# Where the low parts of the local q's weights are made: VectorE's subtraction, or a negation on ScalarE and an accumulating DMA

## The chip, the cores and the metric

The kernel runs on one core of one Trainium2 chip. The metric is the device time of one execution in microseconds (us); the kernel before took 945.75 us (median of 3 runs, 945.48 to 945.87). The engines have short names in the rows: PE is TensorE, the matrix engine (PEld is its loading of weights), DVE is VectorE, ACT is ScalarE, POOL is GpSimd, and SP is SyncE, which here only issues DMAs.

## The reference, cut to what matters

Two encoder layers over 256 tokens of width 1024 in float32. Each layer is a half-step feed-forward block, a mixer with two groups of attention heads that share one input projection, and a second half-step feed-forward block. The change touches the mixer's `sq`, the queries of the local (windowed) heads.

```python
def hybrid_mixer(x, cos, sin, mask, w_in, w_out, lam_vec, subln_g, sink, lambda_init):
    h = x @ w_in                      # columns: dq 512, dk 512, dv 512, sq 512, sk 128, sv 128
    dq, dk, dv, sq, sk, sv = ...
    dq, dk = apply_rope(dq), apply_rope(dk)
    y_diff = diff_attention(dq, dk, dv, lam, subln_g, lambda_init)
    sq, sk = apply_rope(sq), apply_rope(sk)
    y_swa = swa_sink_attention(sq, sk, sv, sink, mask)
    return concatenate([y_diff, y_swa]) @ w_out

for l in range(DEPTH):                # DEPTH = 2
    x = layer_norm(ALPHA * x + 0.5 * swiglu(x, ffn1_w_in[l], ffn1_w_out[l]), ...)
    x = layer_norm(ALPHA * x + hybrid_mixer(x, ..., w_in[l], w_out[l], ...), ...)
    x = layer_norm(ALPHA * x + 0.5 * swiglu(x, ffn2_w_in[l], ffn2_w_out[l]), ...)
```

## The kernel before

Every product is made from two parts of each operand: a high part, rounded to the matrix engine's format `float32r`, and a low part, the difference. A product is then three matmuls: high by high, high by low, low by high.

The weights come in pieces of 128 rows by 1024 columns (512 KB), 158 for each layer (index `i` in the list `srcs`, lines 134 to 149). The class `Weights` (line 58) makes piece `i`: SP issues the DMA into `raw` (line 80, 5 buffers), ACT copies `raw` into `wh` with rounding (line 82, 9 buffers), and DVE writes `wl = raw - wh` (line 83, 9 buffers). A piece is asked for 8 pieces before it is used (`LOOK`). So a new piece's `wh` and `wl` may be written only when PE has read the last of the piece that held the buffer before. The copy and the subtraction stand at a low priority for the scheduler that orders ACT and DVE; the order of PE is the order of the code.

In the mixer the order of PE's work is the table `ORDER` (line 48). `P sq 0 1` is one step of the projection of the local queries for the first half of the tokens: two k-tiles, that is one piece of weights, and six matmuls at lines 497 to 499 (`wh`, `wl`, `wh` again for each k-tile). In the list the pieces of `sq` are 80 to 83 in the first layer. Their first readers on PE stand far apart, with steps of `sk`, `dv` and the scores (`S d`, line 544) between them; the second half of the tokens reads the same pieces again later.

POOL has little to do: a power at line 297 in each layer norm and one at line 633 in each mixer's `diff_pv` (two a layer). No DMA is issued from POOL.

Of the kernel before, what the change touches and what calls it, by code (L numbers as in the profile page):

```python
# [9 lines left out]
F32 = mybir.dt.float32  # L10
# [4 lines left out]
ALU = mybir.AluOpType  # L15
# [36 lines left out]
P dv 0 1; T sk 1; G; A 0 0; T sq 0; P sq 1 1; V 0; S s 0; P sq 1 1; A 1 1; P sq 1 1; S s 0; A 1 0; Y 0; P sq 1  # L52
1; V 1; O 0 2; T sq 1; O 0 2; S s 1; B 0 0; B 0 1; Y 1; W 0 0; W 0 1; S s 1; O 1 1; O 0 4; B 1 0; B 1 1; O 1 2;
W 1 0; W 1 1; Z; O 1 5
"""


class Weights:


    def __init__(self, tc, pool, srcs):
        self.tc, self.nc, self.pool, self.srcs = tc, tc.nc, pool, srcs
        self.made = []

    def _make(self, i):
        nc = self.nc
        raw = self.pool.tile([P, 1024], F32, tag="raw", name=f"raw{i}", bufs=5)
        wh = self.pool.tile([P, 1024], F32R, tag="wh", name=f"wh{i}", bufs=9)
        wl = self.pool.tile([P, 1024], F32R, tag="wl", name=f"wl{i}", bufs=9)

        n = 512 if i < 3 else 1024
        src = self.srcs[i]

        rows = src if isinstance(src, tuple) else (src,)
        for c in range(0, 1024, n):
            s = slice(c, c + n)
            for q, r in enumerate(rows):
                h = P // len(rows)

                (nc.sync if i or c else nc.scalar).dma_start(raw[q * h : (q + 1) * h, s], r[:, s])  # L80
            with self.tc.high_priority(0 if i < 3 else -LATER):
                nc.scalar.copy(wh[:, s], raw[:, s])  # L82
                nc.vector.tensor_tensor(wl[:, s], raw[:, s], wh[:, s].bitcast(F32), ALU.subtract)  # L83
        self.made.append((wh, wl))

    def upto(self, n):
# [9 lines left out]
def encoder_kernel(  # L96
# [22 lines left out]
    nc = tc.nc  # L119
# [3 lines left out]
    wp = ctx.enter_context(tc.tile_pool(name="wp", bufs=1))  # L123
# [7 lines left out]
    dv = nc.vector  # L131


    srcs = []
    for l in range(DEPTH):
        srcs += [f1_b[l, k] for k in range(KT)]
        srcs += [f1_in[l, j, s] for j in range(JT - NB) for s in range(2)]
        srcs += [f1_out[l, k * P : (k + 1) * P, :] for k in range(JT)]
        for c in range(3):
            srcs += [m_in[l, c, q] for q in range(4)]  # L140
        srcs += [m_in2[l, q] for q in range(2)]
        srcs += [m_in[l, 3, q] for q in range(4)]
        srcs += [m_out[l, k * P : (k + 1) * P, :] for k in range(KT // 2)]

        srcs += [tuple(m_out[l, 512 + 256 * v + HD * n : 512 + 256 * v + HD * (n + 1), :] for v in range(2))
                 for n in range(KT // 2)]
        srcs += [f2_b[l, k] for k in range(KT)]
        srcs += [f2_in[l, j, s] for j in range(JT - NB) for s in range(2)]
        srcs += [f2_out[l, k * P : (k + 1) * P, :] for k in range(JT)]
    W = Weights(tc, wp, srcs)  # L150
    wi = 0


# [13 lines left out]
    def load_xt(k0, k1):  # L167
        k = slice(k0, k1)
        xr = tp.tile([P, 2, k1 - k0, P], F32, tag="tmp", name=f"xr{k0}")
        nc.sync.dma_start(xr, x_tr[:, :, k, :])  # L170
        xv = xr.rearrange("p t k c -> p k t c")
        dv.tensor_copy(xx[:, k, 0], xv)
        dv.tensor_tensor(xx[:, k, 1], xv, xx[:, k, 0].bitcast(F32), ALU.subtract)


    for k0, k1 in ((0, 1), (1, 2), (2, 4), (4, 6), (6, 8)):
        load_xt(k0, k1)
        W.upto(k1)
    x = []
# [129 lines left out]
    def ffn(l, n, last=False):  # L309
# [4 lines left out]
        def first(ts, mid=None):  # L314

            hp = [[ps.tile([P, 512], F32, tag="b", name=f"hb_{nm}_{t}{s}") for s in range(2)] for t in ts]
            for k in range(KT):
                wh, wl = W.get(wi + k)
                parts = ((0, wh, 0), (0, wl, 1), (1, wh, 2))
# [29 lines left out]
        def col(*js, flip=False):  # L349
# [3 lines left out]
            for j in js:  # L353

                hs = [ps.tile([P, 2, SEQ], F32, tag="b", name=f"h{'gu'[s]}_{nm}_{j}") for s in range(2)]
                tl = tp.tile([P, 2, SEQ], F32, tag="tl", name=f"tl_{nm}_{j}", bufs=2)
                ws = [W.get(wi), W.get(wi + 1)]
                wi += 2
# [67 lines left out]
        for k in range(JT - TAIL):  # L426
            w = W.get(wi)
            wi += 1
# [432 lines left out]
```

## Time and profile before

| | |
|---|---|
| median of 3 runs | 945.75 us (945.48 to 945.87) |
| the profiled execution | 946.11 us |
| its span, first to last instruction | 944.3 us |
| PE busy | 936.2 us (99%) |
| DVE busy | 657.2 us (70%) |
| ACT busy | 527.2 us (56%) |
| POOL busy | 18.8 us (2%) |
| DMA, mean over the span | 187 GB/s, 176.28 MB in all |

How to read it: the profiled execution's time is 1.8 us longer than its span, which is what lies ahead of the first and behind the last recorded instruction. Busy shares are averages over the whole span; what one stage waits for is read from rows of that stage. In the rows of a timeline the columns are start, duration, engine, line, operation, tiles (output, then inputs), shapes and count, and in brackets the idle time before it with the engine that ended it.

### The profile page before, as it was taken

What the parts mean: (1) busy time and instruction counts of PE and PEld (TensorE: products, weight loads), DVE (VectorE), ACT (ScalarE), POOL (GpSimd) and SP (SyncE); (2) the same over time, 40 slices, a digit from 0 to 9 for tenths busy, and PEclk for the clock granted to TensorE, in tenths of its full rate; (3) what the DMA queues carried; (4) which work ended last, traced back from release to release, by engine and by line L of the source; (5) the groups of instructions that cost most, each with busy time, mean ns of one, the idle gap of its engine ahead of it and who ended that gap; (6) DMA issues with size and microseconds to landing.
All of it is one profiled execution on the core that took longest, in us unless ns stands there. A gap on an engine that the chain in (4) does not pass through costs nothing.

```text
span 944.3 us, 13556 instructions
## 1 busy us (share of the span) xinstructions
PE 936.2 (99%) x5030; PEld 798.8 (85%) x5030; DVE 657.2 (70%) x1089; ACT 527.2 (56%) x906; POOL 18.8 (2%) x27
## 2 busy tenths in 40 slices
PE   9999999999999999999999999999999999999996
PEld 7888888888878888888889888888888889888885
DVE  6787664599887666664586666647998976666635
ACT  5768653346965666643346655543478656556520
POOL 0000000000100000000000000000001000000000
PEclk9999999999999999999999999999999999999999
DMA  8985676366526766676375666763763375666721
GB/s 311 317 274 179 185 227 193 119 235 171 145 73 200 238 179 183 196 223 200 115 247 197 196 184 198 222 189 112 240 175 112 108 238 182 191 193 193 214 66 44
DMA packets 51377, 176.28 MB, mean 187 GB/s; under 512 B 6512, under 2 KB 8304, under 8 KB 51312
## 3 DMA queue, kind: packets, MB, share of 16 engines
q1 hardware_dynamic: 51024, 175.03, 59.1%
q8 instruction: 39, 0.64, 0.3%
q10 hardware_dynamic: 288, 0.39, 0.1%
q14 instruction: 26, 0.21, 0.1%
HBM read 174.35 MB, written 1.05 MB: 186 GB/s over the span
## 4 chain that ended last, share of the span: by engine, by line
PE 99%; DVE 1%; issue 0%; DVEq 0%
PE acc L424 25%; PE hg L364 14%; PE hu L364 14%; PE hb L326 9%; PE hu L369 7%; PE hg L369 7%; PE ao L719 5%; PE pj_sq L497 1%; PE ss L544 1%; PE os L655 1%; PE pj_sq L499 1%; PE pj_sq L498 1%; PE pj_dq L497 1%; PE pj_dq L498 1%; PE tps L611 1%; PE pj_dv L499 1%
## 5 line engine op out<-in xcount | busy, mean ns | idle before, releaser
L83 DVE TENSOR_TENSOR wl<-raw,wh 128x1024 fp32r<-128x1024 f32 (+1 forms) x319 | 385.1, 1210 | 187.5 <-ACT wh L82 106.9
L82 ACT CAST wh<-raw 128x1024 fp32r<-128x1024 f32 (+1 forms) x319 | 332.9, 1047 | 211.2 <-PE acc L424 124.4
L424 PE MATMUL acc<-wh,g 128*128 128x512 f32 (+1 forms) x710 | 191.8, 388 | 0.0
L424 PEld LDWEIGHTS acc<-wh,g 128*128 128x128 f32 x710 | 132.9, 188 | 27.1
L364 PE MATMUL hg<-xx,wh 128*128 128x512 f32 x576 | 143.1, 390 | 0.0
L364 PE MATMUL hu<-xx,wh 128*128 128x512 f32 x576 | 142.3, 389 | 0.0
L364 PEld LDWEIGHTS hu<-xx,wh 128*128 128x128 f32 x576 | 108.1, 188 | 22.5
L364 PEld LDWEIGHTS hg<-xx,wh 128*128 128x128 f32 x576 | 106.6, 188 | 21.2
L424 PE MATMUL acc<-wl,g 128*128 128x512 f32 (+1 forms) x355 | 110.9, 387 | 0.0
L369 PE MATMUL hg<-xx,wl 128*128 128x256 f32 x576 | 81.0, 283 | 0.0
L369 PE MATMUL hu<-xx,wl 128*128 128x256 f32 x576 | 80.9, 283 | 0.0
L424 PEld LDWEIGHTS acc<-wl,g 128*128 128x128 f32 x355 | 66.7, 188 | 13.6
L369 PEld LDWEIGHTS hg<-xx,wl 128*128 128x128 f32 x576 | 75.4, 191 | 1.6
L369 PEld LDWEIGHTS hu<-xx,wl 128*128 128x128 f32 x576 | 74.3, 192 | 0.0
L326 PE MATMUL hb<-wh,xx 128*128 128x512 f32 x256 | 71.1, 396 | 0.0
L379 ACT COPY tl<-hg 128x256 f32<-128x256 f32 x72 | 26.8, 372 | 59.7 <-PE hg L364 57.9
L326 PEld LDWEIGHTS hb<-wh,xx 128*128 128x128 f32 x256 | 48.4, 190 | 10.4 <-ACT wh L82 0.3
L380 DVE TENSOR_TENSOR tl<-hg,tl 128x256 f32<-128x256 f32 x72 | 30.1, 418 | 27.1 <-ACT tl L379 27.1
L385 ACT CAST g<-tl 128x256 fp32r<-128x256 f32 x72 | 29.3, 407 | 23.7 <-DVE tl L383 23.7
L326 PE MATMUL hb<-wl,xx 128*128 128x512 f32 x128 | 39.8, 393 | 0.0
L379 ACT COPY tl<-hu 128x256 f32<-128x256 f32 x72 | 26.6, 370 | 20.0 <-PE hu L369 17.3
L719 PE MATMUL ao<-wh,xx 128*128 128x512 f32 x128 | 36.9, 397 | 0.0
(186 smaller groups left out, 951.1 us busy)
## 6 DMA issues: line engine op xcount, KB each, us to landing
raw<-in_f_in_dram SPq DMA_DIRECT2D x144, 512.0 KB, 4.4
raw<-in_f_out_dram SPq DMA_DIRECT2D x88, 512.0 KB, 4.3
raw<-in_m_in_dram SPq DMA_DIRECT2D x36, 512.0 KB, 4.1
raw<-in_f_b_dram SPq DMA_DIRECT2D x29, 512.0 KB, 3.4
raw<-in_m_out_dram SPq DMA_DIRECT2D x8, 512.0 KB, 4.3
raw<-in_m_out_dram SPq DMA_DIRECT2D x16, 256.0 KB, 5.0
lng<-in_ln_g_dram SPq DMA_DIRECT2D x6, 512.0 KB, 4.7
lnb<-in_ln_b_dram SPq DMA_DIRECT2D x6, 512.0 KB, 5.8
```

What stands on the lines that cost most here:

```text
L82: nc.scalar.copy(wh[:, s], raw[:, s])
L83: nc.vector.tensor_tensor(wl[:, s], raw[:, s], wh[:, s].bitcast(F32), ALU.subtract)
L326: mm(hb[s], xx[:, k, g, t, :], ww[:, 512 * s : 512 * s + 512], start=(k == 0 and e == 0), stop=(k == KT - 1 and e == 2))
L364: mm(hs[s], ws[s][0][:, k * P : (k + 1) * P], xx[:, k], start=(k == 0 and not flip), stop=(k == KT - 1 and flip), skip_group_check=flip)
L369: mm(hs[s][:, 1, :], ws[s][1][:, k * P : (k + 1) * P], xx[:, k, 0], start=(k == 0 and flip), stop=(k == KT - 1 and not flip), skip_group_c ...
L379: nc.scalar.copy(tl[:, s], hs[s][:, 1, :])
L380: dv.tensor_tensor(tl[:, s], hs[s][:, 0, :], tl[:, s], ALU.add)
L385: nc.scalar.copy(gs[q][:, jj, 0, :], gv)
L424: mm(a, g, ww[:, s], start=(k == k0 and e == 0), stop=(k == k1 - 1 and e == 2))
L497: mm(o, xx[:, k, 0, t, :], wh[:, s], start=(k == 0), stop=False)
L498: mm(o, xx[:, k, 0, t, :], wl[:, s], start=False, stop=False)
L719: mm(acc[t][h], xx[:, k, g, t, :], ww[:, s], start=(k == 0 and e == 0), stop=(k == KT - 1 and e == 2))
```

## The change

For the four pieces of `sq` in each layer (a set `by_dma` of their indices) the subtraction on DVE is gone. In its place ACT writes `wl = -raw`, rounded to `float32r` as `wh` is, and POOL then issues a DMA that reads the same 512 KB of weights from memory a second time and adds them onto `wl` where it stands. All other pieces are made as before.

```diff
@@ class Weights, _make
                 nc.scalar.copy(wh[:, s], raw[:, s])
-                nc.vector.tensor_tensor(wl[:, s], raw[:, s], wh[:, s].bitcast(F32), ALU.subtract)
+                if i in self.by_dma:
+
+                    nc.scalar.mul(wl[:, s], raw[:, s], -1.0)
+                    nc.gpsimd.dma_start(wl[:, s], src, accum_op=ALU.add)
+                else:
+                    nc.vector.tensor_tensor(wl[:, s], raw[:, s], wh[:, s].bitcast(F32), ALU.subtract)
...
@@ encoder_kernel
         srcs += [m_in2[l, q] for q in range(2)]
+        by_dma |= set(range(len(srcs), len(srcs) + 4))
         srcs += [m_in[l, 3, q] for q in range(4)]
...
-    W = Weights(tc, wp, srcs)
+    W = Weights(tc, wp, srcs, by_dma)
```

The first place is ACT's queue in the first layer's mixer, where pieces 80 to 83 are made. `raw80`, `wh80`, `wl80` are the buffers of piece 80; `dkT` and `dqT` are the transposed keys and queries of the differential heads, `vs` the local values, `ed` the exponentials. In brackets stand the semaphores waited for. Before:

```order
L82 CAST wh80_1952<-raw80_1951 128x1024 [waits DMAHW4_49,PE_49]
L535 CAST dkT00_1871<-tq_0_dk1_2076 128x4x128 [waits PE_49]
L535 CAST dkT00_1871<-tq_0_dk0_2090 128x4x128 [waits PE_49]
L535 CAST dqT00_1869<-tq_0_dq0_2083 128x4x128
L82 CAST wh81_2004<-raw81_2003 128x1024 [waits DMAHW5_49,PE_49]
L82 CAST wh82_2010<-raw82_2009 128x1024 [waits DMAHW6_49,PE_49]
L82 CAST wh83_2065<-raw83_2064 128x1024 [waits DMAHW7_49,DVE_49,PE_49]
L695 COPY vs0_1876<-pj_0_sk0_2097 128x128 [waits DVE_49,PE_49]
L561 ACT_TABLE_LOAD
```

And the same stretch of ACT now (line numbers are 5 or 6 higher):

```order
L82 CAST wh80_1952<-raw80_1951 128x1024 [waits DMAHW4_49,PE_49]
L85 ACTIVATE wl80_1953<-raw80_1951 128x1024
L541 CAST dkT00_1871<-tq_0_dk1_2080 128x4x128 [waits PE_49]
L541 CAST dkT00_1871<-tq_0_dk0_2094 128x4x128 [waits PE_49]
L541 CAST dqT00_1869<-tq_0_dq0_2087 128x4x128
L85 ACTIVATE wl81_2006<-raw81_2004 128x1024 [waits DMAHW5_49,PE_49]
L82 CAST wh81_2005<-raw81_2004 128x1024 [waits PE_49]
L85 ACTIVATE wl82_2013<-raw82_2011 128x1024 [waits DMAHW6_49,PE_49]
L82 CAST wh82_2012<-raw82_2011 128x1024 [waits PE_49]
L85 ACTIVATE wl83_2069<-raw83_2067 128x1024 [waits DMAHW7_49,DVE_49,PE_49]
L82 CAST wh83_2068<-raw83_2067 128x1024 [waits PE_49,Activation_49]
L701 COPY vs0_1876<-pj_0_sk0_2101 128x128 [waits DVE_49,PE_49]
```

Four negations have come in; for piece 80 the negation follows the cast, for pieces 81 to 83 it stands ahead of it. No load of a table has come in with them.

The second place is PE's queue, at the first readers of `wl80` to `wl83` (`pj_0_sq0` is the projection of the local queries for the first half of the tokens). Before:

```order
L498 MATMUL pj_0_sq0_2249<-wl80_1953,xx_78 128x512
L498 MATMUL pj_0_sq0_2249<-wl81_2005,xx_78 128x512
L498 MATMUL pj_0_sq0_2249<-wl82_2011,xx_78 128x512
L498 MATMUL pj_0_sq0_2249<-wl83_2066,xx_78 128x512
L498 MATMUL pj_0_sq1_2457<-wl80_1953,xx_78 128x512
```

Now:

```order
L504 MATMUL pj_0_sq0_2253<-wl80_1953,xx_78 128x512 [waits DMASW0_49]
L504 MATMUL pj_0_sq0_2253<-wl81_2006,xx_78 128x512 [waits DMASW1_49]
L504 MATMUL pj_0_sq0_2253<-wl82_2013,xx_78 128x512 [waits DMASW2_49]
L504 MATMUL pj_0_sq0_2253<-wl83_2069,xx_78 128x512 [waits DMASW3_49]
L504 MATMUL pj_0_sq1_2461<-wl80_1953,xx_78 128x512
```

The order of PE is the same; the first reader of each piece now waits for the landing of a DMA that POOL issues (`DMASW0` to `DMASW3`, one semaphore for each). On POOL the four DMAs stand between the power of line 297 and the first power of line 633, each behind a wait for its negation on ACT. On DVE the four subtractions are taken out, and the four maxima at line 555 of the first scores stand in another order among themselves. On SP the order is the same; the loads of pieces 84 and 86 to 88 now wait for ACT, where they waited for DVE. The second layer shows the same.

## Rows read from the trace of the kernel before

**Rows 1.** The page's head, its busy time by engine, and the chain that ended last, by engine.

```profile
span 944.3 us, 13556 instructions
PE 936.2 (99%) x5030; PEld 798.8 (85%) x5030; DVE 657.2 (70%) x1089; ACT 527.2 (56%) x906; POOL 18.8 (2%) x27
...
PE 99%; DVE 1%; issue 0%; DVEq 0%
```

**Rows 2.** Busy time by stretch of the span: the stretch, its length, then each engine's busy time with its count of instructions, the granted clock, the DMA engines' busy share and GB/s. The head, the first mixer, the tail, and the sum over the whole span.

```profile
0.00:8.00 8.00, 7.01 (x19) 4.04 (x20) 2.66 (x7) 3.34 (x5) 1.64 (x11) 1.00 0.72 218
...
190.00:262.00 72.00, 72.00 (x442) 61.06 (x441) 65.35 (x133) 46.93 (x115) 3.93 (x3) 1.00 0.60 182
...
935.00:944.30 9.30, 2.17 (x19) 1.97 (x17) 6.09 (x13) 0.00 (x0) 0.92 (x1) 0.89 0.16 56
sum 944.30, PE 936.19 PEld 798.79 DVE 657.25 ACT 527.22 POOL 18.82; mean PE 133.74 PEld 114.11 DVE 93.89 ACT 75.32 POOL 2.69
```

**Rows 3.** Groups of instructions by form: line, engine, operation, tiles and shapes, count, busy us, mean ns, idle before.

```profile
L83 DVE TENSOR_TENSOR wl<-raw,wh 128x1024 fp32r<-128x1024 f32 x313 | 381.0, 1220 | 186.7 <-ACT wh L82 106.1 <-issue 70.5 <-PE hg L369 6.4
L82 ACT CAST wh<-raw 128x1024 fp32r<-128x1024 f32 x313 | 329.2, 1055 | 206.4 <-PE acc L424 124.4 <-PE hu L364 17.1 <-PE hg L364 12.1
...
L381 ACT ACTIVATE tl<-tl 128x256 f32<-128x256 f32 x72 | 30.1, 418 | 7.4 <-DVE tl L380 7.4
...
L385 ACT CAST g<-tl 128x256 fp32r<-128x256 f32 x72 | 29.3, 407 | 23.7 <-DVE tl L383 23.7
```

**Rows 4.** Timeline of ACT in the first mixer, where the casts of pieces 80 to 83 stand (the rows of line 82), and what follows them.

```profile
210.98 1.06 ACT L82 CAST wh<-raw 128x1024 fp32r<-128x1024 f32 x1 [0.30 <-PE pj_dq L499]
212.78 0.59 ACT L535 CAST dkT<-tq_dk 128x512 fp32r<-128x512 f32 x1 [0.75 <-PE tq_dk L533]
...
215.76 1.06 ACT L82 CAST wh<-raw 128x1024 fp32r<-128x1024 f32 x1 [1.02 <-PE pj_dq L499]
217.86 1.06 ACT L82 CAST wh<-raw 128x1024 fp32r<-128x1024 f32 x1 [1.04 <-PE pj_dq L499]
220.01 1.05 ACT L82 CAST wh<-raw 128x1024 fp32r<-128x1024 f32 x1 [1.10 <-PE pj_sk L499]
221.49 0.27 ACT L695 COPY vs<-pj_sk 128x128 f32<-128x128 f32 x1 [0.43 <-DVE m_sk L516]
221.77 1.28 ACT L561 ACT_TABLE_LOAD   x1
223.37 0.48 ACT L561 ACTIVATE ed<-sd,mxd 128x256 f32<-128x256 f32 x1 [0.32 <-DVE mxd L555]
```

**Rows 5.** Timeline of PE: the first readers of `wl80`, `wl81`, `wl82` and `wl83` in the first layer, and the second scores between the last two; then the first two of the second layer.

```profile
222.96 0.39 PE L498 MATMUL pj_sq<-wl,xx 128*128 128x512 f32 x1
...
225.79 0.40 PE L498 MATMUL pj_sq<-wl,xx 128*128 128x512 f32 x1
...
232.73 0.39 PE L498 MATMUL pj_sq<-wl,xx 128*128 128x512 f32 x1
...
233.99 1.70 PE L544 MATMUL sd<-dkT,dqT 64*128 64x256 f32 x24
...
236.34 0.39 PE L498 MATMUL pj_sq<-wl,xx 128*128 128x512 f32 x1
...
689.27 0.39 PE L498 MATMUL pj_sq<-wl,xx 128*128 128x512 f32 x1
...
692.10 0.40 PE L498 MATMUL pj_sq<-wl,xx 128*128 128x512 f32 x1
```

**Rows 6.** Timeline of ACT in the second mixer: the casts of the first and the second piece of `sq`.

```profile
677.28 1.06 ACT L82 CAST wh<-raw 128x1024 fp32r<-128x1024 f32 x1 [0.30 <-PE pj_dq L499]
...
682.06 1.05 ACT L82 CAST wh<-raw 128x1024 fp32r<-128x1024 f32 x1 [1.02 <-PE pj_dq L499]
```

**Rows 7.** Instructions of line 80, the loads of weights: the time from issue to landing, minimum, median and maximum; the first line for the whole span, the second for 195 to 240 us.

```profile
DMA to landing us min/median/max: 2.9/4.3/8.3
...
DMA to landing us min/median/max: 3.3/4.5/7.6
```

**Rows 8.** Busy time by stretch in the first mixer, columns as in rows 2.

```profile
210.00:215.00 5.00, 5.00 (x33) 4.43 (x32) 5.00 (x8) 3.39 (x5) 0.00 (x0) 1.00 0.50 176
215.00:220.00 5.00, 5.00 (x36) 4.61 (x35) 4.92 (x7) 2.11 (x2) 0.00 (x0) 1.00 0.72 220
220.00:225.00 5.00, 5.00 (x48) 4.48 (x48) 5.00 (x10) 4.20 (x10) 0.00 (x0) 1.00 0.81 243
```

**Rows 9.** Timeline of POOL around the first mixer: the last power of the layer norm ahead of it, and the two powers of `diff_pv`.

```profile
194.03 1.00 POOL L297 TENSOR_TENSOR rs<-rs,mhalf 128x1 f32<-128x1 f32 x1 [9.97 <-DVE rs L296]
246.81 1.02 POOL L633 TENSOR_TENSOR f<-f,mhalf 128x4 f32<-128x4 f32 x1 [51.78 <-DVE f L632]
257.40 1.92 POOL L633 TENSOR_TENSOR f<-f,mhalf 128x4 f32<-128x4 f32 x1 [9.57 <-DVE f L632]
```

**Rows 10.** Timeline of DVE in the first mixer: the subtractions of pieces 80 and 81 (one row), 82 and 83, and the first maxima of the scores.

```profile
215.56 2.51 DVE L83 TENSOR_TENSOR wl<-raw,wh 128x1024 fp32r<-128x1024 f32 x2
...
219.19 1.21 DVE L83 TENSOR_TENSOR wl<-raw,wh 128x1024 fp32r<-128x1024 f32 x1
...
221.32 1.21 DVE L83 TENSOR_TENSOR wl<-raw,wh 128x1024 fp32r<-128x1024 f32 x1
...
222.65 2.48 DVE L555 TENSOR_REDUCE mxd<-sd 128x2 f32<-128x512 f32 x4
```

More of the change, by code (lines that the diff above doesn't have):

```diff
@@ L58, with __init__ @@
 class Weights:
-    def __init__(self, tc, pool, srcs):
-        self.tc, self.nc, self.pool, self.srcs = tc, tc.nc, pool, srcs
+    def __init__(self, tc, pool, srcs, by_dma):
+        self.tc, self.nc, self.pool, self.srcs, self.by_dma = tc, tc.nc, pool, srcs, by_dma
         self.made = []
@@ L131, in encoder_kernel @@
     dv = nc.vector
-    srcs = []
+    srcs, by_dma = [], set()
     for l in range(DEPTH):
```

## The prediction

> **What bounds the kernel now.** I read the page's head and its chain first: the span is 944.3 us, PE is busy for 936.2 us of it, and the chain that ended last is 99% PE [rows 1]. The second view is the busy time by stretch. PE lacks 0.99 us in the first 8 us and 7.13 us in the last 9.3 us [rows 2]. That is 8.12 us, and the sum over the span lacks 944.30 - 936.19 = 8.11 us. So between 8 and 935 us PE is never idle, in the first mixer too: 72.00 of 72.00 us, at a granted clock of 1.00 (2.4 GHz). The third view, the timelines of the mixer, is for what PE takes in there and when it is ready.
>
> From this follows what the change can do. It removes no matmul. A DVE that is done earlier gives PE nothing, since PE waits for nobody where the change stands; and a `wl` that is ready after its first reader's turn is paid in full, microsecond for microsecond.
>
> **The change part by part.**
>
> *Off DVE.* Eight subtractions of 1.22 us go [rows 3], 9.8 us of DVE's 657. In the first mixer they are the rows at 215.56 (pieces 80 and 81), 219.19 and 221.32 [rows 10]. Worth to the end: 0. It can't be below 0 either, because head and tail, where PE does wait, hold none of these pieces. What was late next behind them, the maxima at 222.65 [rows 10], can start some tenths sooner.
>
> *Onto ACT.* Eight negations of 128x1024. None is in the trace. The cast of this shape takes 1.055 us, and on 128x256 an ACTIVATE takes 418 ns where a cast takes 407 [rows 3], so I take 1.055 + 0.011 = 1.07 us; the ends are 1.05 (as a cast) and 2.1 (twice that). By the order shown with the change, piece 80's negation follows its cast: the cast ends at 212.04 [rows 4], the negation at 213.11, which pushes the cast of `dkT` from 212.78 by 0.33 us. Pieces 81 to 83 are negated ahead of their casts. I keep the starts at which the buffers came free, 215.76, 217.86 and 220.01 [rows 4]: negation of 81 from 215.76 to 216.83, cast to 217.89; negation of 82 to 218.96, cast to 220.02; negation of 83 to 221.09, cast to 222.15 instead of 221.06. Behind that stand `vs`, the table load and the exponentials, which start about 0.6 us later than 223.37 at most. They feed the transposed query and the second scores, which PE begins at 233.99 [rows 5], ten microseconds later. The cast of `wh81` ends 1.07 us later than before, at 217.89; its first reader stands directly ahead of the row at 225.79. Worth to the end: 0. ACT's cover is its idle time: 15 - 3.39 - 2.11 - 4.20 = 5.3 us in 210 to 225 [rows 8], against 4.3 us added. At 2.1 us each the exponentials would start 5 us late, still ahead of 233.99.
>
> *Onto POOL and the DMA engines.* Four DMAs for each mixer, each issued when its negation ends. POOL stands idle from 194.03 + 1.00 to 246.81 [rows 9], so nothing is queued behind the waiting DMAs but the power at 246.81, and the last negation ends at 221.09. The room from the end of the negation to the first reader [rows 5]:
> - piece 80: 222.96 - 213.11 = 9.85 us
> - piece 81: 225.79 - 216.83 = 8.96 us
> - piece 82: 232.73 - 218.96 = 13.77 us
> - piece 83: 236.34 - 221.09 = 15.25 us
>
> In the second layer the same sums give 689.27 - (677.28 + 1.06 + 1.07) = 9.86 and 692.10 - (682.06 + 1.07) = 8.97 us [rows 5, 6]. So piece 81 has the least room, and a DMA that lands in under 8.96 us costs nothing.
>
> How long it takes no row shows: no DMA is issued from POOL and none adds. The nearest row is the plain load of the same 512 KB, with a median of 4.5 us from issue to landing in this stretch [rows 7]. Added to it: a second pass, since what stands in `wl` must be read too. From 220 to 225 us the DMA engines moved 243 GB/s at a share of 0.81 [rows 8], that is 300 GB/s at full share, so 512 KB are 1.75 us. And POOL's part of the issue, for which the nearest rows are POOL's own operations of 1.0 us [rows 9]. The value I take: 4.5 + 1.75 + 1.0 = 7.25 us (an estimate from these rows). Landings: 220.4, 224.1, 226.2 and 228.3, ahead of the readers by 2.6, 1.7, 6.5 and 8.0 us. The lower end is the fastest load, 2.9 us; the upper end is twice the slowest load and POOL's longest operation, 2 x 8.3 + 1.9 = 18.5 us [rows 7, 9]. A landing ahead of time gains nothing, so the term's ends are 0 and 2 x (18.5 - 8.96) = 19.1 us.
>
> Rows 7 show 3.3 to 7.6 us for loads that SP issues. The Trainium skill, page "DMA: Bandwidth & Descriptors", section "Anatomy of one DMA — SWDGE (gpsimd) path", gives a DMA issued from GpSimd about 2.0 us plus its bytes over 436 GB/s; that would be 3.2 us for 512 KB (an estimate by that page). The Trainium skill, page "Collectives: The Full Stack", section "The bandwidth ceiling: the fold count and why AG ≠ RS ≠ AR", says that an add in the DMA engine needs two source reads and so runs at about half the rate of a copy; by both together the DMA would take 4.4 us and the sum would be the same. No run here shows either yet, and the loads of this stretch are slower than the first page's figure.
>
> *On the loads of SP.* They keep their order. Those of pieces 84 and 86 to 88 now wait for ACT instead of DVE, at most some tenths off their old times. They will be slowed by the added traffic, but their pieces are weights of the output projection, which PE reads behind all of `sq`. Worth 0.
>
> *The sum.* 0 - 0 + 0 on the profiled execution's 946.11 us, which is 1.81 us longer than its span and 0.36 us above the median of 945.75. Forecast in terms of the median: 945.9 us, a tenth or two left for late landings. A change of 0.2% (1.9 us) is about what a measurement of this kernel can tell from none.
>
> **The rivals.**
>
> 1. *The accumulating DMA lands after its first reader's turn (slower).* The place is `wl81`, in both layers, and the point from which it decides is 8.96 us from negation to landing. For it: the DMA engines are free for only (1 - 0.72) x 5 + (1 - 0.81) x 5 = 2.4 us in 215 to 225 [rows 8], while pieces 80 and 81 bring 2 x 2 x 1.75 = 7.0 us of passes, beside SP's loads of pieces 84 to 88. If the two queues share evenly, the two passes of 3.5 us take 7.0, and the DMA takes 2.75 (the load without its pass) + 7.0 + 1.0 = 10.75 us: `wl81` is 1.8 us late, `wl80` 0.9 us, and as the first stall moves PE's later turns along with it, a layer pays 1.8 us and the kernel 3.6: 949.4 us. Against it: the share of 0.50 in 210 to 215 [rows 8] leaves half of the DMA engines to piece 80's transfer where it begins, and the loads of SP wait for buffers, so they don't fill the queue all the time.
>
> 2. *The add is slow in itself (slower, by more).* At the upper end of 18.5 us piece 81 is 9.5 us late in each layer: 945.75 + 19.1 = 964.9 us. The four could also go one after the other through one queue, which puts pieces 82 and 83 late as well. For it: nothing in the trace shows a DMA that adds. Against it: the slowest plain load of the whole span took 8.3 us [rows 7].
>
> 3. *The freed DVE shortens the mixer (faster).* For it: DVE is busy for 65.35 of 72 us there [rows 2], the fullest stretch of that engine. Against it: PE has no idle time to give back, so the gain is bounded by the 8.11 us outside, which the change doesn't touch. Price 0 to -0.5 us: within 0.2%.
>
> 4. *ACT is late for PE.* If the negation took twice a cast, `wh81` would be done near 219 us for a reader just ahead of 225.79 [rows 5]: 0 us, the same as the forecast.
>
> **How the numbers follow.** The forecast (hidden, with rivals 3 and 4, which are the same time) 0.55; rival 1 0.29, of which 0.04 stays under 0.2%, since a DMA between 8.96 and 9.9 us costs under 1.9 us; rival 2 0.13; a gain over 0.2% from a cause that I don't see 0.03. That gives faster 0.03, same 0.55 + 0.04 = 0.59, slower 0.25 + 0.13 = 0.38. The likeliest case's own range is 945.2 to 946.8. The range for 8 in 10 reaches into the late landings up to a DMA of 14.6 us, 945.75 + 2 x (14.6 - 8.96) = 957.0, and leaves out about 0.10 above and 0.03 below 945.0.
>
> **What the profile of the changed kernel would show.** Right, if PE's busy time between 8 and 935 us has no gap and the readers of `wl80` and `wl81` still start 10 and 9 us behind their negations; if the DMAs from POOL list a median from issue to landing under 8 us; if ACT's negations take 1.05 to 1.1 us. Wrong, if PE lists waits of `pj_sq` for a DMA into `wl` (rival 1 at 1 to 2 us each, first of all on `wl81`; rival 2 at many), or if PE's gaps appear at the scores or at `wh81`, which would be ACT. If the time falls by over 2 us, the reading that PE alone bounds the mixer is wrong.

## The result and the profile after

The changed kernel takes 948.78 us (median of 8 runs, 948.39 to 949.17), the kernel before 945.83 us beside it (8 runs, 945.48 to 946.14). The ratio is 1.0031, with an interval of 1.0021 to 1.0040: slower by 2.95 us. The profiled execution took 948.57 us, its span 946.6 us. Lines 85, 86 and 88 are now the negation, the accumulating DMA and the subtraction; line 504 is what was 498, the product of `xx` with a low part.

The page's head, its busy time by engine, its chain by engine, and the two large DMA queues (packets, MB, the time of the packets as a share of 16 engines' span), to be held against [rows 1]:

```profile
span 946.6 us, 13572 instructions
PE 936.2 (99%) x5030; PEld 798.1 (84%) x5030; DVE 648.7 (69%) x1081; ACT 534.3 (56%) x914; POOL 26.0 (3%) x35
...
q1 hardware_dynamic: 51024, 175.03, 57.2%
q0 software_dynamic: 1152, 4.19, 2.2%
...
PE 93%; DMA 3%; issue 2%; DVE 1%; SPq 1%; ACT 0%; POOL 0%; DVEq 0%; POOLq 0%
```

PE does the same 936.2 us of work; the span is 2.3 us longer, and the chain, 99% PE before, now has DMA in it. The new queue q0 holds the eight adding DMAs; SP's loads are in q1.

Busy time by stretch of the changed kernel, the two mixers (columns as in [rows 2]):

```profile
190.00:262.00 72.00, 71.20 (x432) 59.76 (x431) 59.67 (x125) 49.74 (x118) 7.61 (x7) 1.00 0.73 210
657.00:731.00 74.00, 73.10 (x448) 61.85 (x448) 61.78 (x130) 51.20 (x120) 7.36 (x7) 1.00 0.72 206
```

PE was busy for 72.00 of 72.00 us in the first mixer [rows 2] and now lacks 0.80, then 0.90 in the second, at an undiminished clock of 1.00. Who waited for whom, on PE and on its weight load (total us, times, longest):

```profile
PE pj_sq L504 <- DMA wl<-in_m_in_dram: 1.6, 2, 0.9
...
PEld pj_sq L504 <- DMA wl<-in_m_in_dram: 2.6, 3, 1.2
```

The timeline of PE around the first readers of `wl80` and `wl81`, which answers to [rows 5]: the matmul ahead of the first reader of `wl80` in the kernel before, then the changed kernel in the first layer and in the second.

```profile
222.65 0.47 PE L497 MATMUL pj_sq<-wh,xx 128*128 128x512 f32 x1
...
222.34 0.47 PE L503 MATMUL pj_sq<-wh,xx 128*128 128x512 f32 x1
222.91 0.50 PE L504 MATMUL pj_sq<-wl,xx 128*128 128x512 f32 x1
...
225.60 0.39 PE L503 MATMUL pj_sq<-wh,xx 128*128 128x512 f32 x1
226.70 0.50 PE L504 MATMUL pj_sq<-wl,xx 128*128 128x512 f32 x1 [0.70 <-DMA wl<-in_m_in_dram]
...
690.33 0.40 PE L504 MATMUL pj_sq<-wl,xx 128*128 128x512 f32 x1
...
694.22 0.50 PE L504 MATMUL pj_sq<-wl,xx 128*128 128x512 f32 x1 [0.90 <-DMA wl<-in_m_in_dram]
```

The first reader of `wl80` stood 222.96 - 222.65 = 0.31 us behind the matmul ahead of it, and now stands 222.91 - 222.34 = 0.57 behind: `wl80` cost 0.26 us. Within a step these matmuls follow each other every 0.23 us (225.60 should be followed at 225.83), so `wl81` cost 226.70 - 225.83 = 0.87. In the second layer the two readers were 692.10 - 689.27 = 2.83 us apart before; now 694.22 - 690.33 = 3.89, 1.06 more. Together 2.19 us, most of the span's 2.3. The two needn't be equal: PE came to this place 0.31 us earlier than before (222.34 against 222.65), and another 0.4 us lies in small delays between and behind these readers, which were not followed up.

The waits end where the DMAs land. POOL's timeline (the issues of pieces 80 and 81), then line 86 read by windows that hold one issue each: all eight, then pieces 80, 81, 82 and 83 of the first layer.

```profile
213.00 1.05 POOL L86 DMA_DIRECT2D wl<-in_m_in_dram  x1 [18.28 <-ACT wl L85]
216.59 0.87 POOL L86 DMA_DIRECT2D wl<-in_m_in_dram  x1 [2.54 <-ACT wl L85]
...
DMA to landing us min/median/max: 9.5/10.8/13.6
...
DMA to landing us min/median/max: 9.9/9.9/9.9
...
DMA to landing us min/median/max: 10.1/10.1/10.1
...
DMA to landing us min/median/max: 11.9/11.9/11.9
...
DMA to landing us min/median/max: 13.6/13.6/13.6
```

213.00 + 9.9 = 222.9, where `wl80` is first read; 216.59 + 10.1 = 226.7, where `wl81` is. The four land about 3.8 us apart (222.9, 226.7, 230.6, 234.5), while the last three are issued only 2.1 to 2.3 us apart: they come in one after the other. Pieces 82 and 83 take longest and cost nothing: they are read at 233.75 and 237.36.

The other side of the collision is on the page's list of DMA issues (KB each, median us from issue to landing):

```profile
raw<-in_m_out_dram SPq DMA_DIRECT2D x8, 512.0 KB, 10.6
wl<-in_m_in_dram POOLq DMA_DIRECT2D x8, 512.0 KB, 10.8
```

SP's plain loads of the first four output pieces, issued beside them, had a median of 4.3 us before and have 10.6 now. They also start sooner: the first two went out at 213.87 and 216.84 us before, and now both are out by 213.55, since the buffer `raw80` comes free with the negation (212.7) and no longer with the subtraction (216.8). SP's timeline, the second of these loads, before and after:

```profile
216.84 0.33 SPq L80 DMA_DIRECT2D raw<-in_m_out_dram  x1
...
213.55 0.33 SPq L80 DMA_DIRECT2D raw<-in_m_out_dram  x1
```

The busy time by stretch, to be held against [rows 8], shows the DMA engines at that time:

```profile
215.00:220.00 5.00, 5.00 (x37) 4.68 (x36) 2.30 (x4) 4.42 (x5) 1.73 (x2) 1.00 0.88 241
220.00:225.00 5.00, 4.90 (x45) 4.11 (x44) 3.26 (x7) 4.97 (x13) 0.87 (x1) 1.00 1.05 265
225.00:230.00 5.00, 4.29 (x22) 3.42 (x21) 4.10 (x13) 3.40 (x11) 0.00 (x0) 1.00 1.05 275
```

The DMA engines are full from 220 to 230 (the share adds up the times of packets, so it can pass 1). The last number but one of a row for 210 to 240 is 0.65 in the kernel before and 0.94 after:

```profile
210.00:240.00 30.00, 30.00 (x199) 25.89 (x198) 27.83 (x47) 21.16 (x51) 0.00 (x0) 1.00 0.65 178
```

```profile
210.00:240.00 30.00, 29.20 (x193) 24.80 (x192) 22.66 (x41) 23.28 (x51) 3.65 (x4) 1.00 0.94 246
```

One adding DMA takes 2.2% of 946.6 us over eight, 2.60 us of all 16 engines; a plain 512 KB takes 57.2% of 946.6 us x 0.524 / 175.03 MB = 1.62 us. Before, 0.65 x 30 = 19.5 us were used; four adds bring 10.4: 29.9 of 30 us. By this sum the stretch had just about room for the bytes; what it shows is 0.94, 28.2 us.

### The profile page after: what moved, and what is told of

The parts are those of the page before. It is cut to its first block, busy times and chain, and to the rows that moved or that the text cites. A ratio compares the mean times of both kernels' runs of the same rounds, so it can differ in the third digit from the quotient of the medians.

```text
span 946.6 us, 13572 instructions
## 1 busy us (share of the span) xinstructions
PE 936.2 (99%) x5030; PEld 798.1 (84%) x5030; DVE 648.7 (69%) x1081; ACT 534.3 (56%) x914; POOL 26.0 (3%) x35
## 3 DMA queue, kind: packets, MB, share of 16 engines
q1 hardware_dynamic: 51024, 175.03, 57.2%
HBM read 178.55 MB, written 1.05 MB: 190 GB/s over the span
## 4 chain that ended last, share of the span: by engine, by line
PE 93%; DMA 3%; issue 2%; DVE 1%; SPq 1%; ACT 0%; POOL 0%; DVEq 0%; POOLq 0%
PE acc L430 25%; PE hg L370 14%; PE hu L370 14%; PE hb L332 8%; PE hu L375 7%; PE hg L375 7%; PE ao L725 5%; DMA wl<-in_m_in_dram 2%; PE ss L550 1%; PE os L661 1%; PE tps L617 1%; PE od L631 1%; PE pj_sq L504 1%; DMA xr<-in_x_tr_dram 1%; PE pj_sq L505 1%
## 5 line engine op out<-in xcount | busy, mean ns | idle before, releaser
L88 DVE TENSOR_TENSOR wl<-raw,wh 128x1024 fp32r<-128x1024 f32 (+1 forms) x311 | 375.1, 1209 | 189.6 <-ACT wh L82 108.5
L430 PEld LDWEIGHTS acc<-wl,g 128*128 128x128 f32 x355 | 66.7, 188 | 13.6
L332 PEld LDWEIGHTS hb<-wh,xx 128*128 128x128 f32 x256 | 48.0, 189 | 10.4 <-ACT wh L82 0.5
## 6 DMA issues: line engine op xcount, KB each, us to landing
raw<-in_m_out_dram SPq DMA_DIRECT2D x8, 512.0 KB, 10.6
wl<-in_m_in_dram POOLq DMA_DIRECT2D x8, 512.0 KB, 10.8
```

The source lines that it names most:

```text
L332: mm(hb[s], xx[:, k, g, t, :], ww[:, 512 * s : 512 * s + 512], start=(k == 0 and e == 0), stop=(k == KT - 1 and e == 2))
L430: mm(a, g, ww[:, s], start=(k == k0 and e == 0), stop=(k == k1 - 1 and e == 2))
```

## The experiments

The theory after the result: the loss is the late landing of the accumulating DMAs at `wl80` and `wl81`, because they share the DMA engines with SP's loads. The rivals: the work given to ACT and taken from DVE costs it; the add is slow in itself, with no neighbour; the four wait for each other in their queue; each DMA from POOL has a cost of its own. Twelve kernels ran; diffs are against the changed kernel unless it is said otherwise.

**1. Which pieces.** Only pieces 82 and 83 made by DMA, then only 80 and 81.

```diff
-        by_dma |= set(range(len(srcs), len(srcs) + 4))
+        by_dma |= set(range(len(srcs) + 2, len(srcs) + 4))   e1_last_two
+        by_dma |= set(range(len(srcs), len(srcs) + 2))       e2_first_two
```

> Only the last two of the four pieces (82 and 83 and their twins in the second layer) get their low part by the accumulating DMA; 80 and 81 are subtracted on VectorE as before. Theory L (late landing: the whole loss is the wait of the first readers of pieces 80 and 81 on TensorE, because their DMAs from POOL take 9.5 to 13.6 us and the room is 9 to 10): pieces 82 and 83 have 13.8 and 15.2 us of room, so no wait, TensorE without a gap in the mixers, time within 0.5 us of the kernel before (945.8), though the DMAs still take 9 us or more. Rival T (the traffic itself costs: other loads are slowed and something else waits): half the traffic, about half of the loss, 947.2. Rival A (the negations on ACT and the new order on VectorE cost): also about half, 947.2.

> Only the first two pieces (80 and 81) by the accumulating DMA. Theory L: these two are the whole loss, so the time stays within 1 us of the changed kernel's 948.8; a little lower (948) if the DMAs of 82 and 83, issued 2 and 4 us after that of 81, lengthen its landing. Rivals T and A: half of the loss, 947.2.

Measured: e1 946.12 us, ratio 1.0002 (0.9993 to 1.0011); e2 949.01 us, 1.0032 (1.0020 to 1.0044). The whole loss sits at the first two pieces. In e1 the two DMAs landed after 9.5 and 10.9 us in the first layer, longer than a plain load by far, and cost nothing. In e2 piece 81 took 10.5 us in the first layer and 10.7 in the second though nothing stood behind it in POOL's queue, so it does not wait for pieces 82 and 83. Whether it waits for piece 80, which is ahead of it in the queue, no run tests by itself, for none has piece 81 alone; but in e1 the first DMA, with none ahead of it in this stretch, took 9.5 us in the first layer (8.7 in the second) beside SP's loads.

**2. Without the DMA.** The negation stays on ACT, the DMA is left out.

```diff
-                    nc.gpsimd.dma_start(wl[:, s], src, accum_op=ALU.add)
```

> The negation on ACT stays and the DMA is left out, so the low parts of the four pieces hold only the negated high part. Theory L: no wait on a DMA is left, TensorE has no gap in the mixers, 945.8 us within 0.5. Rival A: the negations on ACT and the order of VectorE are still there, so the time stays at 948 to 949. Rival T: 945.8 too.

Measured: 945.98 us, ratio 1.0002 (0.9993 to 1.0010). ACT's negations and DVE's freed time are worth nothing between them; the loss is the DMA's.

**3. The reader later.** One block of another product is put ahead of `wl81`'s first reader in PE's order, some 1.4 us.

```diff
-1; P sq 0 1; P sk 1 2; P sq 0 1; P dv 1 1; P dv 0 3; ...
+1; P sq 0 1; P sk 1 2; P dv 1 1; P sq 0 1; P dv 0 3; ...
```

> The changed kernel with one step of TensorE's order moved: the step that reads piece 81 first comes after one step of the differential values (six matmuls, 1.36 us) instead of ahead of it. Theory L: the room of piece 81 grows by 1.36 us, the wait on its DMA (0.7 and 0.9 us idle in the profile, 0.96 and 1.06 us later than the turn) goes to nearly nothing, the wait on piece 80 (0.27 us in the first layer) stays: 946 to 947 us. Rivals T and A: nothing changes, 948 to 949.

Measured: 946.59 us, ratio 1.0010 (1.0001 to 1.0019): 2.2 of the 2.95 us are back, although the DMAs landed later still, with a median of 11.2 us. The one wait of PE for them that is left is `wl80`'s, in the first layer:

```profile
PE pj_sq L504 <- DMA wl<-in_m_in_dram: 0.8, 1, 0.8
```

**4. Copying in place of adding.** The same DMA, from the same queue, without the add.

```diff
-                    nc.gpsimd.dma_start(wl[:, s], src, accum_op=ALU.add)
+                    nc.gpsimd.dma_start(wl[:, s], src)
```

> The DMAs from POOL stay, at the same places and of the same size, but copy the weights instead of adding them, so the low parts hold the whole weights. It tells what the add costs from what a DMA from POOL costs. Theory L1 (the DMA engines are shared with SP's loads, and the add's second pass over them makes it late): one pass less, 1.75 us or, shared, up to 3.5 us less, so the median from issue to landing falls from 10.8 to 7 to 9 us and the waits are gone: 945.8 to 946.2. Theory L2 (a DMA from POOL is slow whatever it does: its issue, its queue): the landing stays at 10 to 11 us and the time at 948 to 949.

Measured: 946.21 us, ratio 1.0004 (0.9995 to 1.0013), and `wl81` landed 6.9 us after its issue in both layers. The copying kernel's page, its q0 and the same two groups of DMA issues:

```profile
q0 software_dynamic: 1152, 4.19, 1.4%
...
raw<-in_m_out_dram SPq DMA_DIRECT2D x8, 512.0 KB, 7.3
wl<-in_m_in_dram POOLq DMA_DIRECT2D x8, 512.0 KB, 7.4
```

A copying DMA takes 1.4% x 943.7 / 8 = 1.65 us of the engines, as a load of SP's does; the add takes 2.60, 1.6 times that. With a copy the collision is still there (loads at 7.3 us in place of 4.3), but the landing stays under the room of 8.96 us.

**5. The add where nothing waits.** In the kernel before, four extra DMAs from POOL into an unread tile, outside the mixer's crowded stretch: one adding and one copying in each layer.

```diff
+        if add:
+            nc.gpsimd.dma_start(dl, m_in[l, 3, q], accum_op=ALU.add)
+        else:
+            nc.gpsimd.dma_start(dl, m_in[l, 3, q])
```

> The kernel before, with four more DMAs of 512 KB from POOL into a buffer that nobody reads, at places where the DMA engines are nearly idle: behind the second power of line 633 and behind the power of the mixer's first layer norm, one of each pair adding and one copying (adding at the first place in layer one, at the second place in layer two). It measures the DMA by itself. Theory L1 (sharing): alone, an adding DMA lands 6 to 7.5 us after its issue and a copying one 4 to 5.5. Theory L3 (the add is slow in itself): 9.5 us or more for the adding ones even here, under 6 for the copying ones. Theory L2 (POOL's queue is slow): 9 us or more for both. The kernel's own time should not change (945.8 within 0.6).

Measured, in a single run, 946.5 us. Landings of the two adding and then of the two copying DMAs, and q0's packets, MB and share of the 16 engines in 10 us for each (the adds from 259 and from 744 us, the copies from 277 and from 726):

```profile
DMA to landing us min/median/max: 5.8/6.7/7.7
...
DMA to landing us min/median/max: 3.6/4.3/5.0
...
q0 software_dynamic: 144, 0.52, 33.5%
q0 software_dynamic: 144, 0.52, 31.6%
...
q0 software_dynamic: 144, 0.52, 17.1%
q0 software_dynamic: 144, 0.52, 19.2%
```

The places were less quiet than expected, with the engines half to three quarters busy (shares of 0.54 to 0.74). The adds' mean is 2.4 us above the copies', and its slower case, 7.7 us, is still inside 8.96. So the add alone would not have lost the time. In engine time an add took 3.35 and 3.16 us here and a copy 1.71 and 1.92, so 1.8 times; the 1.6 times of experiment 4 holds beside SP's loads. There are two samples of each.

**6. SP's loads held back.** All loads of the output pieces but one wait until `wl81` is in, by a one-column copy on POOL (SP's queue issued one at 213.38 us and the next at 223.73).

```diff
+        if i - 4 in self.by_dma and i - 5 not in self.by_dma:
+            with self.tc.high_priority(-LATER):
+                nc.gpsimd.tensor_copy(raw[:, 0:1], self.made[i - 3][1][:, 0:1].bitcast(F32))
```

> The loads of the output projection's weights behind the four pieces, all but one, are held back until piece 81's DMA has landed: POOL copies one column of its low part into the next load's buffer first, which SP's queue then has to wait for. Theory L1 (sharing with SP's loads makes the DMA late): the landings of pieces 80 and 81 fall from 9.5 to 11 us to 7 to 8.5, the waits go, 945.8 to 946.3 (the held loads have 20 us of room). Theory L3 (the add is slow in itself): the landings stay at 9.5 or more, 948 to 949. POOL stands at the copy meanwhile, so piece 83's DMA is issued some 3 us later, with 15 us of room.

Measured: 952.14 us, ratio 1.0069 (1.0056 to 1.0082). The time went the wrong way, but the landing did what the theory says: `wl81` took 7.0 us in both layers in place of 10.1 and 9.9 (`wl80` 8.8 and 8.3), and no reader of a `wl` waited for a DMA any more. PE has another wait instead, and DVE's timeline shows where it comes from:

```profile
PE tpd L620 <- DVE skT L545: 4.8, 2, 2.9
```

```profile
235.55 1.23 DVE L91 TENSOR_TENSOR wl<-raw,wh 128x1024 fp32r<-128x1024 f32 x1 [2.50 <-ACT wh L85]
236.69 0.28 DVE L545 TENSOR_TENSOR skT<-tq_sk,skT 128x128 fp32r<-128x128 f32 x1
```

DVE stands at line 91, the subtraction of an output piece whose load was held, and behind it in DVE's order stands `skT`, for which PE waits. In the second layer the stall of 2.9 us cost more than itself: behind it the granted clock was 0.50 (1.2 GHz), and the matmuls stood 0.42 us apart in place of 0.23.

```profile
706.46 0.67 PE L620 MATMUL tpd<-ident,ed 128*128 128x128 f32 x4 [2.91 <-DVE skT L545]
...
707.36 0.63 PE L507 MATMUL pj_sq<-wl,xx 128*128 128x512 f32 x1
707.78 0.63 PE L508 MATMUL pj_sq<-wh,xx 128*128 128x512 f32 x1
...
707.00:710.00 3.00, 3.00 (x10) 2.35 (x9) 2.06 (x5) 2.96 (x12) 0.00 (x0) 0.50 1.04 253
```

In these 3 us that is 3 x (1 - 0.23 / 0.42) = 1.4 us. The same fall followed a stall of 2.8 us in e7 and in e13 below, so the traced times of e7, e8 and e13 hold some 1.5 us that are neither a late landing nor a wait. So the prediction's "Worth 0" for SP's loads has a limit as well: they have little slack, not the 20 us that were expected here, and it is used up on DVE, not at PE's readers of those pieces.

**7. The add in halves.** Each accumulating DMA cut into two, by columns (e7), and later by partitions (e14).

```diff
-                    nc.gpsimd.dma_start(wl[:, s], src, accum_op=ALU.add)
+                    for h in range(2):                                    e7_halves
+                        nc.gpsimd.dma_start(wl[:, 512 * h : 512 * h + 512], src[:, 512 * h : 512 * h + 512], accum_op=ALU.add)
...
+                    for b in range(0, P, 64):                             e14_add_rows
+                        nc.gpsimd.dma_start(wl[b : b + 64, :], src[b : b + 64, :], accum_op=ALU.add)
```

> Each accumulating DMA is cut into two of 512 columns, issued one after the other; the first k-tile's reader needs only the first. Theory L1 or L3 (the time is in the moving and adding of the bytes): the first half lands about 2 to 4 us sooner than the whole did, so the wait at piece 81's first reader goes, and the second half is needed 0.7 us later than the first, so a smaller wait may stay there: 946 to 947.5. Theory L2 (a fixed time in issue and completion): both halves land no sooner, two issues of 0.87 us add to it, 949 or more.

> Each accumulating DMA is issued as two of 64 partitions with all 1024 columns, in place of two of 512 columns as in the run with halves that took 954.33 us. Theory F (there the small packets cost the accumulating DMAs their share): with packets as large as in the changed kernel the whole of wl81 is in after 9.5 to 11 us from the first issue, 948.3 to 950 us. Rival: each accumulating DMA has a cost of its own (issue on POOL, a start in the queue), so two for one are as bad as the column halves: 11.5 to 12.5 us, 952 to 955 us.

Measured: e7 954.33 us, ratio 1.0094 (1.0081 to 1.0107); e14 952.21 us, 1.0070 (1.0058 to 1.0082). Each half has an issue of its own, 0.8 to 1.2 us on POOL, where the whole took 0.87, so the second half of `wl81` leaves about half a microsecond later and lands after 11.4 us (columns) and 11.1 us (partitions), near 228.5 in both; the whole was in at 226.7. Counted from the first issue, as was expected, `wl81` took 12.0 us in e7's first layer and 11.6 in e14's, 12.5 and 11.2 in the second. Two DMAs for one cost something of their own: e14, whose rows are as long as the whole DMA's, came out near its rival's figure, so short rows are not the whole reason. They are a part of it: beside e7's rows of 2 KB SP's loads had a median of 7.7 us, beside e14's of 4 KB 10.6 (more in experiment 8). Of the two only e7 also lost time to the clock in its trace (0.50 from 698.5 to 701.9 us, some 1.6 us by the sum of experiment 6). Whether the cost of its own lies in POOL's issue or in the queue the two runs don't tell.

**8. The size of SP's packets.** The first four output loads are each issued as two of 512 columns (e11), four of 256 columns (e13), or, as a control, two of 64 partitions (e12).

```diff
+                if i - 4 in self.by_dma:
+                    for b in range(0, 1024, 512):                         e11_col_halves; 256: e13_col_quarters
+                        nc.sync.dma_start(raw[:, b : b + 512], r[:, b : b + 512])
...
+                    for b in range(0, P, 64):                             e12_row_halves
+                        nc.sync.dma_start(raw[b : b + 64, :], r[b : b + 64, :])
+                    continue
```

> The first four loads of the mixer's output weights (the SP loads that run beside the accumulating DMAs) are each issued as two loads of 512 columns, so that their rows in a packet are 2 KB and not 4 KB; bytes and all else as in the changed kernel. Theory F (the DMA engines are full in this stretch and serve the two queues packet by packet, so that a queue's share goes by the size of its packets): the accumulating DMAs get about two thirds, wl81 lands 8.0 to 9.0 us after its issue in place of 10.1, the first readers no longer wait, 945.9 to 946.8 us, and these loads land later than 10.6 us. Theory B (the queues share by bytes, whatever the size of the packets): wl81 at 9.5 to 10.5 us, 948.3 to 949.3 us.

> As the run with two column halves, but four loads of 256 columns (1 KB rows) in place of each of the four loads. Theory F: wl81 lands at 7.2 to 8.2 us, near the 7.0 us that it took with the loads held back; time 945.8 to 946.6 us, unless the loads are now so late that VectorE's subtractions of their low parts stand before the work that TensorE waits for, as when they were held (then 948 to 952 us with that stall on DVE). Theory B: 9.5 to 10.5 us, 948.3 to 949.3 us.

> Control for the column pieces: the same four loads are each issued as two loads of 64 partitions, so that there are as many DMAs as with column halves but the rows in a packet stay 4 KB. Theory F: as the changed kernel, wl81 at 9.5 to 10.5 us and 948.3 to 949.3 us. A theory C, that the share goes by the number of DMAs in flight: the loads get two thirds, wl81 at 11 to 13 us and 950 to 953 us. Theory B: as F.

Measured, with the landing of `wl81` and of the last piece, 83, by layer:

| SP's first output loads | `wl81`, us | `wl83`, us | the adds' median, us | time, us |
|---|---|---|---|---|
| whole, 4 KB rows (changed kernel) | 10.1, 9.9 | 13.6, 13.4 | 10.8 | 948.78 |
| two of 64 partitions, 4 KB rows (e12) | 10.0, 10.5 | 13.4, 13.8 | 11.1 | 950.25 |
| two of 512 columns, 2 KB rows (e11) | 8.8, 9.6 | 11.5, 11.9 | 9.8 | 950.83 |
| four of 256 columns, 1 KB rows (e13) | 8.2, 9.0 | 9.7, 10.5 | 9.0 | 951.79 |

More DMAs with the same rows change the landing of the adds hardly at all; shorter rows let the adds land sooner, step by step. That is the direction that packet by packet service gives. The first layer is inside what was expected of `wl81` (e11 8.0 to 9.0, e13 7.2 to 8.2), the second 0.6 and 0.8 us above. The packets themselves show the service. In 222 to 226 us, when both queues have work, these are the packets, MB and share of the adds' queue (q0) and of SP's loads (q1): the changed kernel, e11, e13, and e7, where it is the adds that have rows of 2 KB.

```profile
q0 software_dynamic: 152, 0.55, 69.4%
q1 hardware_dynamic: 152, 0.56, 37.0%
...
q0 software_dynamic: 176, 0.66, 82.0%
q1 hardware_dynamic: 177, 0.33, 24.7%
...
q0 software_dynamic: 190, 0.71, 89.2%
q1 hardware_dynamic: 192, 0.18, 16.7%
...
q0 software_dynamic: 220, 0.40, 54.1%
q1 hardware_dynamic: 212, 0.80, 53.1%
```

In each the two queues move as many packets as one another, to 4%, whatever the packets hold: a queue's share of the bytes goes by the length of its rows, and e7's adds got half the bytes of the loads beside them. And no version wins: e11's 950.83 (ratio 1.0057, 1.0043 to 1.0072) missed its 945.9 to 946.8, e13's 951.79 (1.0060, 1.0048 to 1.0072) is what was expected should the loads be late, and e12's 950.25 (1.0046, 1.0034 to 1.0058) lies above the 948.3 to 949.3 of the theory and in the range of theory C, whose landing of 11 to 13 us it does not have. The longest entry of PE's waits in e11, then in e13:

```profile
PE tpd L620 <- DVE skT L545: 3.1, 2, 1.7
```

```profile
PE tpd L620 <- DVE skT L545: 4.0, 2, 2.8
```

It is the wait of the held loads again: what the adds gain in landing, SP's loads lose, and DVE hands it to PE. In e12 PE's wait is on `wl`, two waits of 2.5 us together against 1.6 in the changed kernel. But the execution with this trace took 948.83 us, the lowest of the five, and no trace shows those at the median; why the control is 1.5 us slower stays open.

## Why the prediction was wrong at its forecast and right in its rival

The range for 8 in 10, 945.0 to 957.0, holds the 948.78 us, since rival 1 was priced into it; the forecast of 945.9 and the likeliest case's own range, 945.2 to 946.8, don't.

- *What bounds the kernel.* Held: PE alone bounds the mixer, and a late `wl` is paid in full. The late readers come to 2.19 us, and the span grew by 2.3.
- *Off DVE, onto ACT.* Held, both 0 (the run without the DMA, 945.98). The negations took 1.057 us in the mean, between the 1.05 and 2.1 given and near the 1.07 taken. ACT's exponentials start at 223.05, no later than the 223.37 of [rows 4], and DVE's maxima begin at 221.32 in place of 222.65 [rows 10]. (The bound at 2.1 us a negation is too high by the prediction's own starts: the last cast then ends at 225.24 in place of 221.06, so the exponentials come at most 4.2 us late, not 5.)
- *The room.* Held: the negation of 81 ends at 216.28, and its reader's turn was at 225.83, 9.55 us later, near the 8.96 worked out.
- *Onto POOL and the DMA engines.* This is the step that failed: "The value I take: 4.5 + 1.75 + 1.0 = 7.25 us". Measured: 9.5, 10.8 and 13.6 us (lowest, median, highest), and 9.9 to 10.1 at `wl81`, where it decides. As a price of the DMA with less traffic about it the value was good (it counts from the negation's end, the figures here from POOL's issue, 0.3 us later): 5.8 and 7.7 us in the quiet places, 7.0 at `wl81` with SP's loads held. What it left out is the share of those loads, 10.1 - 7.0 = 3.1 us. It was put into rival 1 only, at a chance of 0.29 against the forecast's 0.55, since "the loads of SP wait for buffers, so they don't fill the queue all the time". The rows at hand were enough to see that they do: 0.50, 0.72 and 0.81 [rows 8] are 10.2 us of 15, and with the 7.0 us of passes that rival 1 gives pieces 80 and 81 they come to more than the stretch holds.
- *The second pass.* Given 1.75 us of all engines besides the first 1.75; the queues' rows show 2.60 in place of 1.65 beside SP's loads, so 0.95 more, and 1.4 more in the quiet places (experiment 5). The Trainium skill, page "Collectives: The Full Stack", section "The bandwidth ceiling: the fold count and why AG ≠ RS ≠ AR", explains the half rate of a ring's ReduceScatter by the two source reads that an add needs. For an add from memory onto a tile these runs show 1.6 times a copy's engine time in the crowded stretch and 1.8 times in the quiet places, somewhat under twice. The Trainium skill, page "DMA: Bandwidth & Descriptors", section "Anatomy of one DMA — SWDGE (gpsimd) path", has a fit that gives 3.2 us for this size (an estimate by that page). The two quiet copies from POOL here took 3.6 and 5.0 us, those beside SP's loads 6.9 to 9.0.
- *On the loads of SP.* "Worth 0" held for the time, but by luck of the order: they went from 4.3 to 10.6 us, and when they were made later still (experiments 6 and 8) it was they that PE paid for, over DVE. That they would go out "at most some tenths off their old times" was wrong: in the first layer the first four went out 0.9 to 3.3 us sooner, the second at 213.55 in place of 216.84, and so met the first add. By itself that costs nothing (the run without the DMA); what part it has in the late landings no run tells.
- *Rival 1* came true, at its place and nearly at its size: 10.75 us from the negation's end to landing against 226.7 - 216.28 = 10.4 at `wl81`, `wl80` late as well, 3.6 us in all against 2.95 measured (in the trace 2.19 at late readers). The landing came so near partly by luck, for a pass of 3.5 us is in it where the queue's row shows 2.60. It had `wl80` at 0.9 us late (0.26 in the first layer, 0 in the second) and `wl81` at 1.8 in all (0.87 and 1.06 more). It let the two queues share the engines' time evenly; what they shared evenly is the packets, of which the adds' take longer (69.4% of the time against 37.0%, experiment 8).
- *Rival 2*, the add slow in itself, falls for the loss: quiet adds land in time. It has a part, though: a copy beside the same loads would have landed in time too (experiment 4). Neither the add nor the neighbours alone lose the time; together they do. *Rivals 3 and 4*: 0, as given.

No kernel here beats the one before. The nearest with DMAs are those that keep them from PE: only the last two pieces (946.12), or the later reader (946.59).

## What to carry to other kernels

Before work is moved onto the DMA engines, add up the engine time of the stretch in which it lands: busy share times length, plus what is added. Where that comes to the whole stretch, price the landing at the crowded figure, for the new transfer and for the loads beside it, and compare both with the room of their first readers. Where two queues meet in full engines, count their packets: a queue with shorter rows gets fewer bytes. And where PE has no gap, an engine that gets free time pays nothing, while every new source of an operand can only be in time or late.

## What the runs showed of the hardware that was not expected

- An accumulating DMA of 512 KB takes 2.60 us of the 16 DMA engines against 1.65 for a copying one from the same queue (3.16 and 3.35 against 1.71 and 1.92 in quiet places), and about 2.4 us more to landing in a quiet place. POOL's issue row is 0.85 to 1.05 us for it; cut into two, the same bytes land later, not sooner, in both ways that were tried.
- Two queues that meet in full engines move as many packets each (152 and 152, 176 and 177, 190 and 192 in 4 us), so the share went with the length of the rows that a load brings: with SP's rows at 4, 2 and 1 KB, `wl83` in the first layer landed after 13.6, 11.5 and 9.7 us, while twice as many DMAs with 4 KB rows left it at 13.4.
- Behind a stall of PE of 2.9 us (e8) the granted clock was 0.50 for some 3 us, and a matmul that comes every 0.23 us came every 0.42.
